# A hybrid decoder layer in which every attention product is made to span the whole TensorE array

## The chip, the cores and the metric

The kernel runs on one core of one Trainium2 chip. The metric is device time in microseconds (us) of one execution; lower is better. Before the change the median of three executions is 1176.98 us (1176.88 to 1177.14).

## The reference

One layer on 256 tokens of width 2048, all in float32. A first projection makes queries (16 heads of 64), keys and values (4 key/value heads, three branches), gates and the input of a convolution. Cut to what matters here:

```python
h = rms_norm(x, mix_norm_g[l]); proj = h @ w_in[l]
q, kv, gate_logits, conv_in = jnp.split(proj, splits, axis=-1)
k_cmp = compress_tokens(kv[:, :, 0, 0], ...)       # blocks of 32 tokens, stride 16, 2-layer MLP
v_cmp = compress_tokens(kv[:, :, 0, 1], ...)
# per query: softmax(q k / 8 + T5 bias) v for three branches, summed with sigmoid gates:
#   compressed blocks (15 of them), selected blocks of 64, sliding window of 512
attn = gc[..., 0:1] * o_cmp + gc[..., 1:2] * o_sel + gc[..., 2:3] * o_win
conv = conformer_conv(conv_in, ...)                 # GLU, 31-tap causal conv, LayerNorm, swish
x = x + jnp.concatenate([attn, conv], axis=-1) @ w_out[l]
x = x + conv_glu_ffn(rms_norm(x, ffn_norm_g[l]), ...)
return rms_norm(x, final_norm_g)
```

With 256 tokens there are four blocks of 64 and up to 16 are selected, and the window is longer than the sequence, so the selected and the window branch both see every earlier token: two plain causal attentions with their own keys and values.

## The kernel before, in words

**Weights.** Every weight matrix comes in chunks of 128x2048 through the queue of SyncE (`wraw`). ScalarE rounds a chunk to the type fp32r (`wh`, line 108), VectorE subtracts that from the original (`wl`, line 111), and each product of the model is the sum of three fp32r products: high with high, high with low, low with high (`mm3`, lines 133 to 135, 256 columns; `mm_rows`, lines 140 to 142, 512 columns). Splits run two chunks ahead of their use.

**Stages.** TensorE first makes the convolution's inputs, then keys and values of the compressed branch, then the two MLPs of the compression (`cmp_in`, line 420: 16 products of 75 columns with 64 weight columns, once for keys and once for values), the keys of the other two branches (`kt_`, line 465), the values (`vt`, lines 485 and 500), and last eight tiles of queries of two heads each (`tile_chunk`, `q_evac` at line 513). The 30 multiply-adds per channel tile of the 31-tap convolution (line 347, "taps" below) are put on VectorE between all this by `fill`, which compares two rough clocks of the planner, one for TensorE and one for VectorE.

**Attention.** There are 32 units, one for each of 16 heads and 2 branches (`units`). `attn_tick` issues one step of a software pipeline over the units; a tick at number n holds, in this order, the value products of unit n-5 (`st_out`), the transposes of unit n-4 (`st_transpose`), the scores of unit n (`st_scores`), and on the other engines the row minima of unit n-1 (VectorE, `st_min`), the reciprocal of the sums (`st_rec`), the evacuation of the transposes, the scaling and the exponential (ScalarE). Four ticks go into each of the query tiles 2 to 7 and into the first chunks of the output projection, between its weight products. These attention products are in plain fp32, which TensorE runs as two instructions each; they use the array in parts. Scores contract over the 64 channels of one head, so they use 64 rows:

```python
nc.tensor.matmul(s[:, :P], qt[h, i, :P], kt_[h, br, i // 4, :P], start=True, stop=True)
```

Values have 64 channels, so their products use 64 columns, and the product with the compressed values (line 630) uses 64 rows. The transposes and all weight products use all 128 rows and 128 columns. The trace writes this as rows*columns behind the operation (64*128, 128*64, 128*128).

The order on each engine is the order in which the Python code issues the work; `hook` is called four times per chunk and pops side work (`steps`, taps, a tick, a piece of a weight split).

Of the kernel before, what the change touches and what calls it, by code (L numbers as in the profile page):

```python
# [45 lines left out]
def hybrid_trunk(ctx: ExitStack, tc: tile.TileContext, a: dict, out: bass.AP):  # L46
# [134 lines left out]
    xt_l = mixp.tile([P, KD, T], F32R, name="xt_l")  # L181


    with ExitStack() as mx:
# [7 lines left out]
        w1 = ap.tile([P, 2, 16, HD], F32, name="w1", tag="w1")  # L192
        w2 = ap.tile([HD, 2, HD], F32, name="w2")
# [43 lines left out]
        rB = ap.tile([P, T], F32, name="rB1")  # L237
# [43 lines left out]
        def tab_rel():  # L281
            pr = bank[6]
            nc.tensor.matmul(pr[:16, :384], rbn, oh[:, P:], start=True, stop=True)
            rtab = wk.tile([16, 384], F32, name="rtab", tag="es", bufs=2)
            nc.vector.tensor_copy(rtab, pr[:16, :384])
            nc.scalar.dma_start(scratch, rtab)
# [32 lines left out]
        def hook(i, ticks=0):  # L319
# [4 lines left out]
            if ticks > i:  # L324
                attn_tick()
            if i >= 2:
                w_pump(1)
            fill(1.0 if ticks > i else 0.8 if cbst["q"] else 2.0)
# [3 lines left out]
        def tile_chunk(ps, ticks=0):  # L332
# [80 lines left out]
        vc = ap.tile([P, 2, 2, HD], F32, name="vc")  # L413
# [3 lines left out]
        def cmp_in(kv):  # L417
            cm[kv] = ph = bank[4 + kv]
            for i in range(16):
                nc.tensor.matmul(ph[:HD, :75], w1[:, kv, i], tok[:, kv, :, i:i + 113:8],  # L420
                                 start=i == 0, stop=i == 15)

        def cmp_sig(kv):
            ph = cm[kv]
            hb = wk.tile([HD, 1], F32, name="hb")
            nc.vector.tensor_copy(hb, ph[:HD, 60:61])
            sgm = wk.tile([HD, 60], F32, name="sgm", bufs=1)
            nc.scalar.activation(sgm, ph[:HD, :60], AF.Sigmoid, bias=hb)
            cm[kv] = ph, hb, sgm

        def cmp_silu(kv):
            ph, hb, sgm = cm[kv]
            cm[kv] = hd = wk.tile([HD, 4, 32], F32, name="hd")
            nc.gpsimd.memset(hd, 0.0)
            nc.vector.scalar_tensor_tensor(hd[:, :, :NCMP], ph[:HD, :60].rearrange("p (h n) -> p h n", h=4),
                                           hb, sgm.rearrange("p (h n) -> p h n", h=4),
                                           op0=OP.add, op1=OP.mult)

        def cmp_out():
            pk, pv = bank[6:]  # L440
            for r in range(2):
                nc.tensor.matmul(pk[64 * r:64 * r + 64, :2 * NCMP], w2[:, 0], cm[0][:, r::2, :NCMP],
                                 start=True, stop=True)
            for j in range(4):
                for q in range(2):
                    nc.tensor.matmul(pv[32 * j:32 * j + 32, q * HD:(q + 1) * HD], cm[1][:, 2 * q + j % 2],
                                     w2[:, 1], start=True, stop=True)

        def cmp_keep():
# [4 lines left out]
            for j in range(4):  # L454
                sl = slice(32 * j, 32 * j + 32)
                nc.vector.tensor_copy(vc[sl, :, j % 2], pv[sl, :2 * HD].rearrange("p (q n) -> p q n", q=2))

        steps.extend((lambda: None, lambda: None, lambda: cmp_in(0), lambda: None, lambda: cmp_sig(0),
                      lambda: (cmp_in(1), cmp_silu(0)), lambda: None, lambda: cmp_sig(1), lambda: None,
                      lambda: cmp_silu(1), lambda: None, cmp_out, lambda: None, cmp_keep))  # L460

        kt_ = ap.tile([P, 2, 2, T], F32, name="kT")
# [5 lines left out]
        vt = ap.tile([P, 2, 2, 256], F32, name="vt")  # L468
# [15 lines left out]
        for t in range(2):  # L484
            nc.scalar.activation(vt[:, t, 0], vb[t][:, :256], AF.Copy, scale=rc[:, t:t + 1])
# [13 lines left out]
        for t in range(2):  # L499
            nc.scalar.activation(vt[:, t, 1], vb[t][:, :256], AF.Copy, scale=rc[:, t:t + 1])  # L500
# [9 lines left out]
        qt = ap.tile([P, 8, T], F32, name="qT", tag="w1")  # L510
# [525 lines left out]
```

## Time and profile before

| | |
|---|---|
| median of three executions | 1176.98 us |
| the profiled execution | 1177.07 us, of which the span of instructions is 1175.3 us |
| granted TensorE clock, mean | 0.997 of full speed |
| TensorE (PE) busy | 1161.2 us, 99% of the span, 7986 products |
| VectorE (DVE) busy | 788.3 us, 67% |
| ScalarE (ACT) busy | 567.4 us, 48% |

The matmul's ends in the trace are modelled and products overlap in it, so what one product costs TensorE is read from the distance between the starts of neighbours, not from its own duration. The chain of waits does that by itself: its entries add up to the span.

### The profile page before, as it was taken

The page shows a single profiled execution, that of the slowest core. Times are in us where ns is not written, and L with a number is a line of the kernel's source. Part 1 is how long each engine was busy: PE and PEld are TensorE (multiplying, and loading weights), DVE is VectorE, ACT ScalarE, POOL GpSimd, SP SyncE. Part 2 cuts the span into 40 slices and gives each one's busy share as a digit, 9 for nine tenths or more (in the row PEclk, how much of TensorE's full clock was granted, in tenths as well). Part 3 has the DMA queues.
Part 4 walks back from the last instruction along what each step waited for, and adds up shares of the span by engine and source line. Part 5 has one row for each costly group of instructions (what it writes and reads, how often), then busy time and mean ns, then how long its engine had stood idle before and what let it go on. Part 6 is the DMA issues. An engine that isn't in the chain of part 4 may idle for free.

```text
span 1175.3 us, 18945 instructions
## 1 busy us (share of the span) xinstructions
PE 1161.2 (99%) x7986; PEld 1058.1 (90%) x7986; DVE 788.3 (67%) x1192; ACT 567.4 (48%) x770; POOL 6.8 (1%) x25
## 2 busy tenths in 40 slices
PE   8999999999999999999999999999999999999997
PEld 8999999777678899999999999999999888888886
DVE  6889889777665666666766666666667654556544
ACT  6544225666655644444453544444444544444443
POOL 1000000000000000000000000000000000000000
PEclk9999999999999999999999999999999999999999
DMA  9575336222245454554445355545544555555551
GB/s 364 217 294 181 144 104 232 73 72 73 71 180 195 163 215 149 211 190 168 174 187 214 144 209 176 190 155 204 199 160 175 218 182 183 185 205 179 179 178 72
DMA packets 32224, 207.60 MB, mean 177 GB/s; under 512 B 3739, under 2 KB 6123, under 8 KB 7948
## 3 DMA queue, kind: packets, MB, share of 16 engines
q1 hardware_dynamic: 28592, 199.64, 47.1%
q10 hardware_dynamic: 3548, 6.76, 1.6%
q8 instruction: 62, 1.02, 0.3%
q14 instruction: 22, 0.18, 0.0%
HBM read 204.27 MB, written 2.12 MB: 176 GB/s over the span
## 4 chain that ended last, share of the span: by engine, by line
PE 95%; DMA 2%; DVE 1%; ACT 1%; issue 1%; SPq 0%; POOLq 0%; DVEq 0%; POOL 0%; ACTq 0%
PE bank L133 19%; PE bank L134 19%; PE bank L135 19%; PE bank L140 9%; PE bank L142 9%; PE bank L141 9%; PE bank L625 2%; PE bank L611 1%; DMA wraw<-in_w_t 1%; PE bank L570 1%; PE bank L569 1%; DMA hb<-in_head 1%; PE bank L420 1%; PE bank L626 1%; PE bank L630 0%
## 5 line engine op out<-in xcount | busy, mean ns | idle before, releaser
L133 PE MATMUL bank<-xt_h,wh 128*128 128x256 f32 x1920 | 548.1, 285 | 2.6 <-ACT wh L233 2.6
L135 PE MATMUL bank<-xt_h,wl 128*128 128x256 f32 x1920 | 544.8, 284 | 0.5 <-DVE wl L111 0.4
L134 PE MATMUL bank<-xt_l,wh 128*128 128x256 f32 x1920 | 544.5, 284 | 0.0
L111 DVE TENSOR_TENSOR wl<-wraw,wh 128x2048 fp32r<-128x2048 f32 (+2 forms) x239 | 421.3, 1784 | 119.0 <-ACT wh L108 118.9
L108 ACT ACTIVATE wh<-wraw 128x2048 fp32r<-128x2048 f32 (+2 forms) x239 | 352.6, 1500 | 141.0 <-PE bank L142 62.5
L133 PEld LDWEIGHTS bank<-xt_h,wh 128*128 128x128 f32 x1920 | 368.9, 192 | 12.2 <-issue 9.0
L135 PEld LDWEIGHTS bank<-xt_h,wl 128*128 128x128 f32 x1920 | 368.9, 192 | 1.2 <-DVE wl L234 0.6
L134 PEld LDWEIGHTS bank<-xt_l,wh 128*128 128x128 f32 x1920 | 369.0, 192 | 0.0
L844 ACT ACTIVATE yt<-u,vecs 128x256 f32<-128x256 f32 x88 | 53.0, 602 | 204.9 <-DVE u L842 204.9
L142 PE MATMUL bank<-wh,gl 128*128 128x512 f32 (+1 forms) x360 | 140.9, 392 | 0.0
L140 PE MATMUL bank<-wh,gh 128*128 128x512 f32 (+1 forms) x360 | 140.9, 392 | 0.0
L141 PE MATMUL bank<-wl,gh 128*128 128x512 f32 (+1 forms) x360 | 140.9, 391 | 0.0
L847 DVE SCALAR_TENSOR_TENSOR yt<-u,vecs,yt 128x255 f32<-128x255 f32 (+1 forms) x176 | 85.1, 484 | 62.3 <-ACT yt L844 59.1
L347 DVE SCALAR_TENSOR_TENSOR y<-us,cw,y 128x256 f32<-128x256 f32 x240 | 101.2, 479 | 0.4 <-ACT y L350 0.3
L142 PEld LDWEIGHTS bank<-wh,gl 128*128 128x128 f32 x360 | 67.9, 189 | 15.7
L141 PEld LDWEIGHTS bank<-wl,gh 128*128 128x128 f32 x360 | 67.9, 188 | 15.7
L140 PEld LDWEIGHTS bank<-wh,gh 128*128 128x128 f32 x360 | 67.9, 188 | 15.7
L842 DVE TENSOR_TENSOR u<-bank,rB 128x256 f32<-128x256 f32 x88 | 36.9, 420 | 27.1 <-PE bank L135 27.1
L836 ACT ACTIVATE gh<-gt 128x1024 fp32r<-128x1024 f32 x22 | 23.3, 1059 | 64.6 <-PE bank L141 64.6
L837 DVE TENSOR_TENSOR gl<-gt,gh 128x1024 fp32r<-128x1024 f32 x22 | 27.0, 1225 | 41.0 <-ACT gh L836 41.0
L879 ACT ACTIVATE sgf<-yt 128x256 f32<-128x256 f32 x44 | 18.4, 418 | 50.3 <-DVE yt L847 50.3
L880 DVE TENSOR_TENSOR gt<-sgf,yt 128x256 f32<-128x256 f32 x44 | 18.7, 426 | 24.5 <-ACT sgf L879 24.5
(171 smaller groups left out, 795.8 us busy)
## 6 DMA issues: line engine op xcount, KB each, us to landing
wraw<-in_w_u SPq DMA_DIRECT2D x88, 1024.0 KB, 4.9
wraw<-in_w_d SPq DMA_DIRECT2D x44, 1024.0 KB, 4.8
wraw<-in_w_t SPq DMA_DIRECT2D x30, 1024.0 KB, 5.0
wraw<-in_w_o SPq DMA_DIRECT2D x16, 1024.0 KB, 4.9
wraw<-in_w_vg SPq DMA_DIRECT2D x4, 608.0 KB, 3.7
hb<-in_head SPq DMA_DIRECT2D x2, 1024.0 KB, 10.9
xr<-in_x SPq DMA_DIRECT2D x2, 1024.0 KB, 16.6
wb<-rel_scratch ACTq DMA_DIRECT2D x1, 2048.0 KB, 13.0
```

What stands on the lines that cost most here:

```text
L108: nc.scalar.activation(h[:, sl], raw[:, sl], AF.Copy)
L111: nc.vector.tensor_sub(l[:, sl], raw[:, sl], h[:, sl].bitcast(F32))
L133: nc.tensor.matmul(ps, wh, xh, start=first, stop=False)
L134: nc.tensor.matmul(ps, wh, xl, start=False, stop=False)
L135: nc.tensor.matmul(ps, wl, xh, start=False, stop=last)
L140: nc.tensor.matmul(ps, xh, wh, start=first, stop=False)
L141: nc.tensor.matmul(ps, xh, wl, start=False, stop=False)
L142: nc.tensor.matmul(ps, xl, wh, start=False, stop=last)
L347: nc.vector.scalar_tensor_tensor(y[:, j], us[:, j, k:k + T], cw[:, j, k:k + 1], y[:, j], op0=OP.mult, op1=OP.add)
L842: nc.vector.tensor_mul(u, bank[:, :T], rB)
L844: nc.scalar.activation(yt, u, AF.Identity, scale=fcw[:, c, 2:3], bias=fcw[:, c, 3:4])
L847: nc.vector.scalar_tensor_tensor(yt[:, d:], u[:, :T - d], fcw[:, c, k:k + 1], yt[:, d:], op0=OP.mult, op1=OP.add)
```

## The change

Five things change.

1. **Scores.** The queries of a head are stored on all 128 partitions, the fp32r high part on one half and the low part on the other (`qs`); the keys are stored twice, once on each half, as a high tile `k_h` and a low tile `k_l`. One fp32r product then contracts over 128 rows and gives (high + low) times high, a second one adds the rest. Both branches lie side by side in the moving operand, so one call serves two units: four products with 256, 256, 512 and 512 columns.
2. **Values** are zero-padded to 128 columns (`vt` has a block of zeros between the two heads), so a unit's value products write all 128 partitions; the compressed values are padded in the same way over rows (`vc`).
3. **Compression.** The first layers for keys and values run as one product with 128 weight columns and 150 moving columns; only two of its four quarters are used.
4. **New copies.** Each key tile takes one VectorE product, six ScalarE copies and two VectorE subtractions on 64 partitions; each query tile two copies and two subtractions beside its evacuation.
5. **Plan.** The planner's price of a tick falls from 2.5 to 1.4. Ticks start in query tile 1 (two of them), stay at four in tiles 2 to 7, six go into the first chunk of the output projection, the rest into its second chunk. The pipeline of ticks and its order are otherwise as they were.

TensorE, one tick inside a query tile. Before (`kT`, `qT` are keys and queries, `es` the transposed probabilities, `e` the probabilities):

```order
L625 MATMUL bank_71<-es,vt 64x256
L626 MATMUL bank_71<-es,vt 64x128
L611 MATMUL bank_70<-ident,e 128x128 x3
L569 MATMUL bank_68<-kT,qT 128x128
L570 MATMUL bank_68<-kT,qT 128x256
L133 MATMUL bank_65<-xt_h,wh 128x256
```

After, a tick that carries scores (the next tick ends behind its transposes):

```order
L659 MATMUL bank_71<-es,vt 128x256
L660 MATMUL bank_71<-es,vt 128x128
L646 MATMUL bank_70<-ident,e 128x128 x3
L604 MATMUL bank_66<-k_h,qs 128x256
L605 MATMUL bank_66<-k_l,qs 128x256
L604 MATMUL bank_68<-k_h,qs 128x512
L605 MATMUL bank_68<-k_l,qs 128x512
L133 MATMUL bank_65<-xt_h,wh 128x256
```

The sequence is the same; the scores of two units stand together, every second tick has none, and the value products write 128 partitions instead of 64.

VectorE, the end of a query tile. Before (`smc`, `pcb` belong to the compressed branch):

```order
L111 TENSOR_TENSOR wl<-wraw,wh 128x1024
L347 SCALAR_TENSOR_TENSOR y<-us,cw,y 128x256 x3
L513 SCALAR_TENSOR_TENSOR qT<-bank_64,rB_191 128x256
L544 TENSOR_REDUCE smc<-ec 128x8
L545 RECIPROCAL smc<-smc 128x8
L546 TENSOR_TENSOR smc<-smc,gates 128x8
```

After:

```order
L111 TENSOR_TENSOR wl<-wraw,wh 128x1024
L348 SCALAR_TENSOR_TENSOR y<-us,cw,y 128x256 x2
L535 SCALAR_TENSOR_TENSOR q_2736<-bank_64,rB 128x256
L539 TENSOR_TENSOR qs<-q_2736,qs 64x256 x2
L570 TENSOR_REDUCE smc<-ec 128x8
L571 RECIPROCAL smc<-smc 128x8
L572 TENSOR_TENSOR smc<-smc,gates 128x8
```

Two subtractions are new behind the evacuation, and each of them reads what ScalarE has just copied; fewer taps stand in the tile (19 in two tiles, where 24 stood).

VectorE, where the taps run out, in the first chunks of the output projection. Before:

```order
L347 SCALAR_TENSOR_TENSOR y<-us,cw,y 128x256 x5
L544 TENSOR_REDUCE smc<-ec 128x8
L545 RECIPROCAL smc<-smc 128x8
L546 TENSOR_TENSOR smc<-smc,gates 128x8
L547 TENSOR_TENSOR pcb<-ec,smc 128x8x15
L633 TENSOR_TENSOR ma_l<-bank_71,ma_h 128x256
L579 ISA e,mn<-bank_69,wb 128x128
L579 ISA mn 128x1
L579 ISA e,mn<-bank_69,wb 128x256
L579 ISA mn 128x1
L662 TENSOR_REDUCE y<-y 128x128
L598 RECIPROCAL lsum<-lsum 128x4
```

After:

```order
L348 SCALAR_TENSOR_TENSOR y<-us,cw,y 128x256 x3
L666 TENSOR_TENSOR ma_l<-bank_71,ma_h 128x256
L614 ISA e,mn<-bank_66,wb 128x128
L614 ISA mn 128x1
L614 ISA e,mn<-bank_69,wb 128x256
L614 ISA mn 128x1
L348 SCALAR_TENSOR_TENSOR y<-us,cw,y 128x256 x18
L633 RECIPROCAL lsum<-lsum 128x4
L634 TENSOR_TENSOR lsum<-lsum,gates 128x4
L695 TENSOR_REDUCE y<-y 128x128 x2
```

Eighteen taps are left when the last row minima are done, and they stand ahead of the reciprocal of the last two units.

The diff, cut to its core (tile declarations, renamed indices and the layout on the host are left out):

```diff
-        def hook(i, ticks=0):
+        def hook(i, ticks={}):
...
-            if ticks > i:
-                attn_tick()
+            if i in ticks:
+                for _ in range(ticks[i]):
+                    attn_tick()
...
-        def cmp_in(kv):
-            cm[kv] = ph = bank[4 + kv]
+        def cmp_in():
             for i in range(16):
-                nc.tensor.matmul(ph[:HD, :75], w1[:, kv, i], tok[:, kv, :, i:i + 113:8],
+                nc.tensor.matmul(bank[4][:, :150], w1[:, i].rearrange("p v d -> p (v d)"), tok[:, :, :, i:i + 113:8],
                                  start=i == 0, stop=i == 15)
...
         for n in range(4):
             tile_chunk(bank[n][:, :T])
-            nc.vector.tensor_mul(kt_[:, n // 2, n % 2], bank[n][:, :T], rB)
+            br, q = divmod(n, 2)
+            k32 = wk.tile([P, T], F32, name="k32", tag="q32", bufs=2)
+            nc.vector.tensor_mul(k32, bank[n][:, :T], rB)
+            for r in range(2):
+                h, o = slice(64 * r, 64 * r + 64), slice(64 - 64 * r, 128 - 64 * r)
+                nc.scalar.activation(k_h[h, r, q, br], k32[h], AF.Copy)
+                nc.vector.tensor_sub(k_l[h, r, q, br], k32[h], k_h[h, r, q, br].bitcast(F32))
+                nc.scalar.activation(k_h[o, r, q, br], k32[h], AF.Copy)
+                nc.scalar.activation(k_l[o, r, q, br], k_l[h, r, q, br].bitcast(F32), AF.Copy)
...
         def q_evac(i, bank):
-            nc.vector.scalar_tensor_tensor(qt[:, i], bank[:, :T], -(HD ** -0.5), rB, op0=OP.mult, op1=OP.mult)
+            q32[i] = wk.tile([P, T], F32, name="q32", tag="q32", bufs=2)
+            nc.vector.scalar_tensor_tensor(q32[i], bank[:, :T], -(HD ** -0.5), rB, op0=OP.mult, op1=OP.mult)
+            for r in range(2):
+                h, o = slice(64 * r, 64 * r + 64), slice(64 - 64 * r, 128 - 64 * r)
+                nc.scalar.activation(qs[h, i % 4, r], q32[i][h], AF.Copy)
+                nc.vector.tensor_sub(qs[o, i % 4, r], q32[i][h], qs[h, i % 4, r].bitcast(F32))
...
+        def st_bank(n):
+            hh = n // 2
+            return bank[2][:, hh % 2 * T:(hh % 2 + 1) * T], bank[4 + hh % 2]
+
         def st_scores(n):
             i, r, br = units[n]
-            h = slice(64 * r, 64 * r + 64)
-            s = bank[4 + n % 2]
-            nc.tensor.matmul(s[:, :P], qt[h, i, :P], kt_[h, br, i // 4, :P], start=True, stop=True)
-            nc.tensor.matmul(s[:, P:384], qt[h, i, P:], kt_[h, br, i // 4], start=True, stop=True)
+            if br:
+                return
+            q, q4 = qs[:, i % 4, r], i // 4
+            for t, s in enumerate(st_bank(n)):
+                sl, ks = slice(t * P, (t + 1) * P), slice(0, (t + 1) * P)
+                nc.tensor.matmul(s, q[:, sl], k_h[:, r, q4, :, ks], start=True, stop=False)
+                nc.tensor.matmul(s, q[:, sl], k_l[:, r, q4, :, ks], start=False, stop=True)
...
         def st_out(n):
             i, r, br = units[n]
             es = US.pop(n)
-            o = bank[7][64 * r:64 * r + 64]
-            c0 = (2 * (i // 4) + r) * HD
+            o, v = bank[7], vt[:, :, br, i // 4, r:r + 2]
             kw = dict(skip_group_check=True)
-            nc.tensor.matmul(o[:, :T], vt[:, 0, br, c0:c0 + HD], es[:, :T], start=br == 0, stop=False, **kw)
-            nc.tensor.matmul(o[:, P:T], vt[:, 1, br, c0:c0 + HD], es[:, T:], start=False, stop=False, **kw)
+            nc.tensor.matmul(o[:, :T], v[:, 0], es[:, :T], start=r + br == 0, stop=False, **kw)
+            nc.tensor.matmul(o[:, P:T], v[:, 1], es[:, T:], start=False, stop=False, **kw)
...
-            clock["pe"] += 2.5
+            clock["pe"] += 1.4
...
+        TICKS = {0: {}, 1: {2: 1, 3: 1}, 2: {0: 1, 1: 1, 2: 1, 3: 1}, 3: {0: 1, 1: 2, 2: 1, 3: 2}}
         for i in range(8):
-            tile_chunk(bank[i % 2][:, :T], ticks=4 if i > 1 else 0)
+            tile_chunk(bank[i % 2][:, :T], TICKS[min(i, 2)])
...
         for n, (qr, g) in enumerate(OUT_ORDER):
-            if n == 2:
+            if n == 1:
+                while cbst["done"] < 4:
+                    step()
                 while tick["n"] < NU + 1:
                     attn_tick()
```

## Rows read from the trace of the kernel before

**Rows 1.** The page's chain that ended last, by engine and by line.

```profile
PE 95%; DMA 2%; DVE 1%; ACT 1%; issue 1%; SPq 0%; POOLq 0%; DVEq 0%; POOL 0%; ACTq 0%
PE bank L133 19%; PE bank L134 19%; PE bank L135 19%; PE bank L140 9%; PE bank L142 9%; PE bank L141 9%; PE bank L625 2%; PE bank L611 1%; DMA wraw<-in_w_t 1%; PE bank L570 1%; PE bank L569 1%; DMA hb<-in_head 1%; PE bank L420 1%; PE bank L626 1%; PE bank L630 0%
```

**Rows 2.** Stretches: start:end, length, busy us per engine, clock, DMA share, GB/s.

```profile
130.00:165.00 35.00, 35.00 (x293) 34.02 (x293) 25.85 (x57) 8.19 (x11) 0.00 (x0) 1.00 0.31 106
165.00:198.00 33.00, 33.00 (x262) 33.00 (x261) 31.80 (x61) 14.42 (x25) 0.00 (x0) 1.00 0.61 219
231.10:263.10 32.00, 32.00 (x198) 23.77 (x198) 23.36 (x80) 21.23 (x64) 0.13 (x1) 1.00 0.19 66
291.00:320.00 29.00, 29.00 (x138) 18.78 (x137) 21.18 (x65) 19.25 (x60) 0.00 (x0) 1.00 0.16 43
320.00:334.00 14.00, 12.61 (x62) 8.25 (x60) 4.81 (x10) 8.73 (x21) 0.00 (x0) 1.00 0.56 214
```

**Rows 3.** Timeline of TensorE, one tick: start us, duration us, what.

```profile
236.00 0.28 PE L134 MATMUL bank<-xt_l,wh 128*128 128x256 f32 x1
236.12 0.28 PE L135 MATMUL bank<-xt_h,wl 128*128 128x256 f32 x1
236.33 0.65 PE L625 MATMUL bank<-es,vt 128*64 128x256 f32 x2
236.81 0.38 PE L626 MATMUL bank<-es,vt 128*64 128x128 f32 x2
237.12 0.55 PE L611 MATMUL bank<-ident,e 128*128 128x128 f32 x3
237.60 0.48 PE L569 MATMUL bank<-kT,qT 64*128 64x128 f32 x2
237.92 0.59 PE L570 MATMUL bank<-kT,qT 64*128 64x256 f32 x2
238.45 0.39 PE L133 MATMUL bank<-xt_h,wh 128*128 128x256 f32 x1
238.67 0.28 PE L134 MATMUL bank<-xt_l,wh 128*128 128x256 f32 x1
```

**Rows 4.** Timeline of TensorE, transposes among 512-column products, later in the kernel.

```profile
390.32 0.39 PE L142 MATMUL bank<-wh,mc_l 128*128 128x512 f32 x1
390.55 0.60 PE L765 MATMUL bank<-ident,x 128*128 128x128 f32 x4
390.91 0.48 PE L140 MATMUL bank<-wh,mc_h 128*128 128x512 f32 x1
391.22 0.40 PE L141 MATMUL bank<-wl,mc_h 128*128 128x512 f32 x1
```

**Rows 5.** The chain in order of time: start us, its share in us, what.

```profile
132.03 4.51 PE bank L420 x32
...
201.27 0.81 PE bank L524 x8
...
202.50 0.43 PE bank L570 x2
```

**Rows 6.** Timeline of TensorE, the next tick, with the compressed values.

```profile
240.55 0.38 PE L626 MATMUL bank<-es,vt 128*64 128x128 f32 x2
240.86 0.70 PE L630 MATMUL bank<-pct,vc 64*128 64x256 f32 x2
241.49 0.33 PE L611 MATMUL bank<-ident,e 128*128 128x128 f32 x1
```

**Rows 7.** TensorE's waits: engine, line, releaser, total us, times, longest.

```profile
PE bank L611 <- ACT ck L690: 1.4, 1, 1.4
```

**Rows 8.** Groups by line in 231.1 to 263.1: count, busy us, mean ns, idle before.

```profile
L347 DVE SCALAR_TENSOR_TENSOR y<-us,cw,y 128x256 f32<-128x256 f32 x24 | 10.2, 480 | 0.0
...
L605 ACT ACTIVATE e<-e,lsum 128x256 f32<-128x256 f32 x8 | 4.0, 499 | 0.0
...
L616 ACT ACTIVATE es<-bank 128x384 f32<-128x384 f32 x8 | 3.9, 490 | 9.1 <-PE bank L611 9.1
...
L598 DVE RECIPROCAL lsum<-lsum 128x4 f32<-128x4 f32 x4 | 0.7, 178 | 4.2 <-ACT e L590 4.1
```

More of the change, by code (lines that the diff above doesn't have):

```diff
@@ L181, in hybrid_trunk @@
     xt_l = mixp.tile([P, KD, T], F32R, name="xt_l")
+    rB = mixp.tile([P, T], F32, name="rB")
     with ExitStack() as mx:
@@ L191, in hybrid_trunk @@
         cw = ap.tile([P, 8, TAPS + 3], F32, name="cw")
-        w1 = ap.tile([P, 2, 16, HD], F32, name="w1", tag="w1")
-        w2 = ap.tile([HD, 2, HD], F32, name="w2")
+        w1 = ap.tile([P, 16, 2, HD], F32, name="w1", tag="w1")
+        w2 = ap.tile([P, HD], F32, name="w2")
         def load_small():
@@ L283, in tab_rel @@
             nc.tensor.matmul(pr[:16, :384], rbn, oh[:, P:], start=True, stop=True)
-            rtab = wk.tile([16, 384], F32, name="rtab", tag="es", bufs=2)
+            rtab = wk.tile([16, 384], F32, name="rtab", tag="e", bufs=4)
             nc.vector.tensor_copy(rtab, pr[:16, :384])
@@ L412, in hybrid_trunk @@
         nc.gpsimd.memset(kc, 0.0)
-        vc = ap.tile([P, 2, 2, HD], F32, name="vc")
+        vc = ap.tile([P, 2, 2, 2, HD], F32, name="vc")
         nc.gpsimd.memset(vc, 0.0)
         cm = {}
-        def cmp_in(kv):
-            cm[kv] = ph = bank[4 + kv]
+        def cmp_in():
             for i in range(16):
-                nc.tensor.matmul(ph[:HD, :75], w1[:, kv, i], tok[:, kv, :, i:i + 113:8],
+                nc.tensor.matmul(bank[4][:, :150], w1[:, i].rearrange("p v d -> p (v d)"), tok[:, :, :, i:i + 113:8],
                                  start=i == 0, stop=i == 15)
         def cmp_sig(kv):
[L424 to L429, printed above, removed]
-        def cmp_silu(kv):
[L432 to L436, printed above, removed]
+            h = slice(64 * kv, 64 * kv + 64)
+            ph = bank[4][h, 75 * kv:75 * kv + 75]
+            hb = wk.tile([P, 1], F32, name="hb")
+            nc.vector.tensor_copy(hb[h], ph[:, 60:61])
+            sgm = wk.tile([P, 60], F32, name="sgm", bufs=2)
+            nc.scalar.activation(sgm[h], ph[:, :60], AF.Sigmoid, bias=hb[h])
+            cm[kv] = h, ph, hb, sgm
+        def cmp_silu(kv):
+            h, ph, hb, sgm = cm[kv]
+            cm[kv] = hd = wk.tile([P, 4, 32], F32, name="hd")
+            nc.gpsimd.memset(hd[h], 0.0)
+            nc.vector.scalar_tensor_tensor(hd[h, :, :NCMP], ph[:, :60].rearrange("p (h n) -> p h n", h=4),
+                                           hb[h], sgm[h].rearrange("p (h n) -> p h n", h=4),
                                            op0=OP.add, op1=OP.mult)
@@ L445, in cmp_out @@
                 for q in range(2):
-                    nc.tensor.matmul(pv[32 * j:32 * j + 32, q * HD:(q + 1) * HD], cm[1][:, 2 * q + j % 2],
-                                     w2[:, 1], start=True, stop=True)
+                    nc.tensor.matmul(pv[32 * j:32 * j + 32, q * HD:(q + 1) * HD], cm[1][HD:, 2 * q + j % 2],
+                                     w2[HD:], start=True, stop=True)
         def cmp_keep():
@@ L651, in attn_tick @@
                 if 0 <= n - d < NU:
-                    assert f is not st_scores or n // 8 < cbst["q"]
+                    assert f is not st_scores or n // 4 in q32
                     f(n - d)
@@ L712, in conf_split @@
             if j0 == 0:
-                cf["o"] = (ap.tile([P, 8, T], F32R, name="mc_h", tag="us"), ap.tile([P, 8, T], F32R, name="mc_l"))
+                cf["o"] = (ap.tile([P, 8, T], F32R, name="mc_h", tag="us"), ap.tile([P, 8, T], F32R, name="mc_l", tag="mc_l"))
             sl = slice(j0, j0 + 4)
@@ L741, in hybrid_trunk, with out_part @@
         x2 = None
-        def out_part(ws, qr, g, t):
+        def out_part(n, ws, qr, g, t):
             wh, wl = ws
@@ L802, in hybrid_trunk @@
         dg = mixp.tile([P, 2, P], F32, name="dg2")
-        rB = mixp.tile([P, T], F32, name="rB")
         def x2_rstd(t):
```

51 lines of the change are left out of this document (28 added, 23 removed).

## The prediction

> **What bounds the kernel now.** I read the chain of waits first. TensorE holds 95% of it, nearly all of it in weight products that the change leaves alone; the lines that it touches hold about 7% [rows 1]. So TensorE's own time is what counts, and the question is what the attention products cost it. The stretches say the same of the stage where they are: in two query tiles TensorE is busy for all of 32.0 us at a granted clock of 1.00 (the upper level, 2.4 GHz), while VectorE has 23.4 us of work and ScalarE 21.2 us [rows 2]. Third comes one tick in TensorE's timeline, where the starts of neighbours give the price of each piece [rows 3]. A weight product of 256 columns takes 0.12 us there, from start to start.
>
> **Array switches.** From the start of L135 to the start of L134 behind the tick 2.55 us pass [rows 3]; two weight products of 0.12 are in that, so the tick takes 2.31 us. The bare price of its contents comes from stretches where nothing changes shape. Four transposes between 512-column products take, with the product behind them, from 390.55 to 391.22, that is 0.67 us; a 512-column product alone takes 0.23 (390.32 to 390.55), so an fp32 pass of 128 columns is 0.11 us [rows 4], and one of 256 columns 0.215 (0.43 for two) [rows 5]. The tick holds 2 x 0.215 + 2 x 0.108 for the values, 3 x 0.108 for the transposes, 2 x 0.108 + 2 x 0.215 for the scores: 1.61 us. The other 0.70 us stand where the shape of the array changes: weight product (128 rows by 128 columns) to values (128 by 64), to transposes (128 by 128), to scores (64 by 128), back to the weight product; four changes of about 0.17 us. Entering transposes from a weight product of the same shape costs nothing [rows 4], nor does leaving them, so it is the shape and not the change from fp32r to fp32 that costs. Afterwards all of it has one shape. Over 32 units: 32 x 0.70 = 22.4 us. Where the compressed values follow, from 240.86 to 241.49 pass 0.63 us for two passes worth 0.43 [rows 6]; eight of these give 8 x 0.20 = 1.6 us more.
>
> **Scores.** Two units cost 2 x 0.646 = 1.29 us of bare passes now. Afterwards they are two fp32r products of 256 and two of 512 columns, 2 x 0.12 + 2 x 0.23 = 0.70 us. Sixteen pairs: 20.7 - 11.2 = 9.5 us.
>
> **Padded values.** The passes have as many columns as before, so they take the same time; only the weights are 128 wide instead of 64. Products of 32 columns behind loads of 128 take 0.10 us each [rows 5], so such a load takes at most 0.10 us; the transposes have loads of that width and run at 0.11 us a pass [rows 4], so the loads hide behind 128 columns, and I take 0 (bounds: 0 to 2 x 0.10 x 32 = 6.4 us, if those behind the two shorter passes came out whole). By the Trainium skill, "TensorE: Matmul & The Clock Gate", section "LDWEIGHTS (loading the stationary operand)", a load goes by its columns, P/1.2 ns: my estimate from it is 107 instead of 53 ns, and were none hidden, four loads in 32 units would take 6.8 us from the sum; the 0.10 us of the row agrees with the duration.
>
> **Compression.** 32 passes of 75 columns take 4.51 us, 0.141 each [rows 5], more than 128 neighbouring columns take (0.11). The moving columns lie eight elements apart. If the time goes by such columns, the 32 passes of 150 take as long as the 64 passes now (9.0 us) and nothing is saved; if it goes by passes, 4.5 us are saved. I take 0, since 75 columns that cost more than 128 are most simply slow columns, and add 0.6 us for the four shape changes around the two visits (at 0.17). By the Trainium skill, "SBUF — State Buffer", section "Door 1: The DMA port swizzle", full rate needs accesses that fall in the same line of 16 bytes, four fp32, and steps beyond that pay for each access: by it too the sum is 0, without it 4.5 us.
>
> **A wait that goes.** TensorE waits 1.4 us once for ScalarE's copy of a convolution mean [rows 7], because that column range shares a bank with the transposes. In the new order the means come behind the last tick: 1.4 us.
>
> TensorE alone: 22.4 + 1.6 + 9.5 + 0.6 + 1.4 = 35.5 us.
>
> **What comes back as waits.** The tick shrinks from 2.31 to (0.646 + 0.324 + 0.35) = 1.32 us, so two tiles shrink from 32.0 to 32.0 - 8 x 0.99 - 0.2 = 23.9 us. VectorE's work there [rows 2]: 23.4, less 5 taps of 0.43, plus 4 half-height subtractions, at the tap's price for want of a row, so 22.9. ScalarE's: 21.2 plus 4 copies at 0.50 = 23.2 [rows 8]. All three engines stand within 1 us. ScalarE's queue used to wait 9.1 us there for transposes, and VectorE's 4.2 us for the exponentials [rows 8]; that slack is what the change spends. Three places can stop TensorE:
> - Tile ends: VectorE evacuates, ScalarE copies, VectorE subtracts, and everything behind that in both queues (row minima, the next weight split, the evacuation of transposes) waits. Hidden, it costs 0; with both copies exposed VectorE needs 22.9 + 2 = 24.9, 1.0 more than TensorE per two tiles, 3 us over six tiles. I take 2.
> - The first output chunk has six ticks among 24 products, twice two in a row, and a seventh follows. A second tick's value products need the evacuation of the transposes just issued. The one exposed step in the trace cost 1.4 us [rows 7]; three of them give 0 to 4.2. I take 2.
> - Eighteen taps, 18 x 0.43 = 7.7 us, stand on VectorE ahead of the last reciprocal, and ScalarE's scaling and TensorE's transposes of the last two units are behind it. TensorE still has two ticks without scores (2 x 0.97) and some nine 512-column products (2.1) before it asks. The cover is 4 us: 0 to 3.7. I take 2.
>
> Copies of the keys: in 130 to 165 VectorE is busy 25.9 of 35 us and ScalarE 8.2 [rows 2], so 12 more operations of 0.43 and 24 copies of 0.50 fit; the next stretch has VectorE at 31.8 of 33, and a lag of 2 or 3 us is carried through it by weight splits that run two chunks ahead. I take 0 (bounds 0 to 3). DMA is busy 0.16 to 0.61 of the time and moves the same bytes.
>
> **Sum.** 35.5 - 6 = 29.5 us off the profiled execution's 1177.07 us (the span of 1175.3 and 1.8 around it; the runs' median of 1176.98 is the same within 0.1): 1147.6 us. With the bounds of the waits, 0 to 10.9, the forecast itself spans 1141.6 to 1152.5.
>
> **Rivals.**
> *VectorE and ScalarE become the bound of attention.* For: work of 22.9 and 23.2 against 23.9 us, in queues that take their work in order; against: in 165 to 198 VectorE already runs at 96% without stopping TensorE [rows 2]. If the 4.2 us per two tiles that VectorE now waits for exponentials stay, VectorE needs 27.1, 3.2 over TensorE, 9.6 over six tiles; with the upper ends of the other two places (7.9) that is 1141.6 + 17.5 = 1159.1. Such runs lie between 1152.5 and 1160.
> *The compression's time goes by passes.* 4.5 us more: 1143.1. For it is only that no row shows two counts of columns at that step.
> *The change does not free the array.* If going between fp32r and fp32, or writing through padded weights, cost the same 0.17 us, three of four changes per tick would stay, 0.52 x 32 = 16.8 us: 1147.6 + 16.8 less the waits that longer ticks would cover (6) is 1158.4. Rows 4 speak against it.
> *Slower.* ScalarE's queue sets the pace of each tick: transposes, evacuation, scaling, next transposes as one loop, exposed in every tick. The place is the wait of the transposes for the scaling; the price is the 1.4 us of the one exposed step [rows 7]. Over 37 ticks that is 51.8 us against a gain of 35.5, so 1193.4; it decides from 0.96 us per tick on. Against it: a loop of one tick needs evacuation and scaling, 0.49 + 0.39 + 0.50 at most, while a tick with its twelve weight products lasts 1.32 + 1.4 = 2.7 us.
>
> **How the numbers follow.** Forecast 66% (1147.6; own range 1141.6 to 1152.5); VectorE and ScalarE as the bound 17% (1152.5 to 1160); compression by passes 8% (1143.1); array not freed 5% (1158.4); slower 4% (1193). A range of 1140 to 1158 leaves out the slower case, most of the array case, a few points of the first rival at its far end and a few of the second with no wait at all: about 2 in 10. About 0.2% (2.4 us) is what a measurement of this kernel can tell from no change. Every case but the last is faster by more than that, and I keep 1% for a mixture of several bad ends: faster 0.95, same 0.01, slower 0.04.
>
> **What would show it.** Right: one tick with scores of about 1.65 us and one without of about 1.0 between weight products in TensorE's timeline; value products marked 128*128 with two passes in 0.65 us together; the stretch of the query tiles 2 to 7 shorter by some 24 us; TensorE's waits on evacuations and probabilities, near absent now, adding up to about 6 us around the first two output chunks and at tile ends; VectorE and ScalarE over 90% busy there; the compression's products still near 9 us. Wrong: starts still 0.2 us late at the edges of a tick (the array), or waits above 11 us in all (VectorE and ScalarE), or a compression of 4.5 us.

## The result, and the profile after

| | before | changed |
|---|---|---|
| median, four executions each | 1177.06 us | 1171.26 us (1169.61 to 1172.36) |
| profiled execution | 1177.07 us | 1169.61 us |
| TensorE busy | 1161.2 us | 1136.2 us |
| VectorE busy | 788.3 us | 797.3 us |
| ScalarE busy | 567.4 us | 582.9 us |

The ratio is 0.9949 with a 95% interval of 0.9937 to 0.9961. The kernel is faster by 5.8 us, half a per cent, where 29.5 were forecast, and the time lies outside the range. TensorE is busy for 25 us less (busy time counts modelled ends, so this is not yet its gain), and the chain shows what took its place. The page's chain that ended last, by engine and by line:

```profile
PE 82%; DVE 11%; ACT 3%; DMA 2%; issue 1%; SPq 0%; DVEq 0%; POOLq 0%; POOL 0%; ACTq 0%
PE bank L133 17%; PE bank L135 17%; PE bank L134 17%; PE bank L140 9%; PE bank L142 9%; PE bank L141 9%; DVE y L348 4%; DVE wl L111 3%; DMA wraw<-in_w_t 1%; DMA hb<-in_head 1%; DVE e L614 1%; PE bank L421 1%; ACT wh L108 1%; PE bank L659 1%; ACT e L625 0%
```

In [rows 1] TensorE held 95% and VectorE 1%; now they hold 82% and 11%, and the first lines of VectorE on the path are the convolution's taps (L348) and the weights' low parts (L111), neither of them touched by the change. The stretches say where (start:end, length, busy us of TensorE, weight loads, VectorE, ScalarE, GpSimd, clock, DMA share, GB/s; those of before are [rows 2]):

```profile
165.00:198.00 33.00, 28.57 (x216) 27.65 (x216) 31.47 (x62) 17.48 (x32) 0.00 (x0) 1.00 0.53 181
204.00:284.00 80.00, 72.40 (x529) 67.21 (x528) 68.90 (x240) 66.10 (x199) 0.38 (x3) 1.00 0.23 80
291.00:320.00 29.00, 23.52 (x118) 19.29 (x117) 23.72 (x70) 18.71 (x57) 0.00 (x0) 0.94 0.10 37
304.00:306.00 2.00, 1.05 (x6) 0.71 (x6) 1.64 (x7) 1.21 (x5) 0.00 (x0) 1.00 0.57 135
306.00:309.40 3.40, 3.40 (x11) 2.94 (x12) 3.40 (x11) 2.26 (x7) 0.00 (x0) 0.51 0.54 229
```

Before, TensorE had no gap in the first four stretches of [rows 2]. Now it lacks 4.4 us in 165 to 198 (the value stage), 7.6 us in 204 to 284 (six query tiles), and 5.5 us in 291 to 320 (the first output chunks), where the clock also stands at its half level (0.51, 1.2 GHz) for 3.4 us, behind 2 us in which TensorE was busy for only 1.05. TensorE's waits by line (total us, times, longest), without those at the start of the kernel; all of them are new:

```profile
PE bank L646 <- ACT e L640: 4.1, 2, 2.6
PE bank L515 <- DVE wl L111: 4.0, 3, 1.8
PE bank L578 <- DVE pcb L573: 3.7, 3, 1.4
...
PE bank L659 <- ACT es L651: 2.0, 6, 0.8
PE bank L550 <- DVE q L535: 1.5, 1, 1.5
PE bank L663 <- ACT pct L580: 1.1, 1, 1.1
```

These six lines alone add up to 16.4 us; the forecast had named more than 11 us of waits as a sign that it was wrong.

The length of the tick came out as forecast. One tick with scores in TensorE's timeline (start us, duration us), which answers to [rows 3]:

```profile
244.25 0.28 PE L135 MATMUL bank<-xt_h,wl 128*128 128x256 f32 x1
244.37 0.59 PE L659 MATMUL bank<-es,vt 128*128 128x256 f32 x2
244.80 0.38 PE L660 MATMUL bank<-es,vt 128*128 128x128 f32 x2
245.02 0.49 PE L646 MATMUL bank<-ident,e 128*128 128x128 f32 x3
245.26 0.37 PE L604 MATMUL bank<-k_h,qs 128*128 128x256 f32 x1
245.47 0.28 PE L605 MATMUL bank<-k_l,qs 128*128 128x256 f32 x1
245.59 0.39 PE L604 MATMUL bank<-k_h,qs 128*128 128x512 f32 x1
245.82 0.39 PE L605 MATMUL bank<-k_l,qs 128*128 128x512 f32 x1
246.05 0.28 PE L133 MATMUL bank<-xt_h,wh 128*128 128x256 f32 x1
```

From 244.37 to 246.05 are 1.68 us (1.65 foreseen), and the values start 0.12 us behind the weight product, as one weight product does behind another: at that edge no change of shape is left. Where the time went is a matter of waits, so I took the starts of the first weight product of each stage from the traces; the differences below are between such starts:

| stretch | before | changed | keys late | keys, queries late | taps last | half taps, means held | fastest order |
|---|---|---|---|---|---|---|---|
| value stage | 24.9 | 30.3 | 24.9 | 24.9 | 30.4 | 27.5 | 24.9 |
| query tiles 2 to 7 | 89.4 | 80.0 | 79.6 | 74.4 | 80.0 | 71.1 | 74.4 |
| first output chunk | 16.3 | 22.0 | 22.0 | 22.2 | 23.3 | 20.6 | 17.2 |
| second output chunk | 17.5 | 14.5 | 15.8 | 14.5 | 9.7 | 11.3 | 10.6 |
| third and fourth | 18.9 | 11.6 | 11.6 | 11.6 | 12.3 | 11.6 | 14.1 |
| whole (median) | 1177.1 | 1171.3 | 1165.0 | 1160.8 | 1167.3 | 1152.0 | 1152.9 |

(us; the columns to the right are the experiments below, and each column is one profiled execution. What follows the fourth output chunk takes 835.3 to 836.7 us in the runs of this table, so the stretches hold nearly all of the difference. The kernel before has its ticks in other chunks, and the fastest order has one of the first output chunk's in the next, so for these two the rows of the output chunks compare only as a sum.)

### The profile page after: what moved, and what is told of

It is laid out like the page before. It is cut to its first block, busy times and chain, and to the rows that moved or that the text cites. A ratio compares the mean times of both kernels' runs of the same rounds, so it can differ in the third digit from the quotient of the medians.

```text
span 1167.8 us, 18821 instructions
## 1 busy us (share of the span) xinstructions
PE 1136.2 (97%) x7890; PEld 1056.6 (90%) x7890; DVE 797.3 (68%) x1216; ACT 582.9 (50%) x810; POOL 7.6 (1%) x26
## 4 chain that ended last, share of the span: by engine, by line
PE 82%; DVE 11%; ACT 3%; DMA 2%; issue 1%; SPq 0%; DVEq 0%; POOLq 0%; POOL 0%; ACTq 0%
PE bank L133 17%; PE bank L135 17%; PE bank L134 17%; PE bank L140 9%; PE bank L142 9%; PE bank L141 9%; DVE y L348 4%; DVE wl L111 3%; DMA wraw<-in_w_t 1%; DMA hb<-in_head 1%; DVE e L614 1%; PE bank L421 1%; ACT wh L108 1%; PE bank L659 1%; ACT e L625 0%
## 5 line engine op out<-in xcount | busy, mean ns | idle before, releaser
L111 DVE TENSOR_TENSOR wl<-wraw,wh 128x2048 fp32r<-128x2048 f32 (+2 forms) x239 | 421.2, 1782 | 120.4 <-ACT wh L108 120.2
L348 DVE SCALAR_TENSOR_TENSOR y<-us,cw,y 128x256 f32<-128x256 f32 x240 | 101.0, 477 | 0.6 <-ACT y L351 0.3
L142 PEld LDWEIGHTS bank<-wh,gl 128*128 128x128 f32 x360 | 67.8, 188 | 15.8
L141 PEld LDWEIGHTS bank<-wl,gh 128*128 128x128 f32 x360 | 67.8, 188 | 15.8
L140 PEld LDWEIGHTS bank<-wh,gh 128*128 128x128 f32 x360 | 67.8, 188 | 15.8
L872 ACT ACTIVATE gh<-gt 128x1024 fp32r<-128x1024 f32 x22 | 23.3, 1059 | 64.6 <-PE bank L141 64.6
L915 ACT ACTIVATE sgf<-yt 128x256 f32<-128x256 f32 x44 | 18.4, 418 | 49.7 <-DVE yt L883 49.7
L916 DVE TENSOR_TENSOR gt<-sgf,yt 128x256 f32<-128x256 f32 x44 | 18.7, 425 | 23.9 <-ACT sgf L915 23.9
```

The source lines that it names most:

```text
L111: nc.vector.tensor_sub(l[:, sl], raw[:, sl], h[:, sl].bitcast(F32))
L140: nc.tensor.matmul(ps, xh, wh, start=first, stop=False)
L141: nc.tensor.matmul(ps, xh, wl, start=False, stop=False)
L142: nc.tensor.matmul(ps, xl, wh, start=False, stop=last)
L348: nc.vector.scalar_tensor_tensor(y[:, j], us[:, j, k:k + T], cw[:, j, k:k + 1], y[:, j], op0=OP.mult, op1=OP.add)
```

## The experiments

The diffs in this section are shortened.

My first theory was that VectorE is late from the keys on; the rival was that the copies through ScalarE and the loop of a tick set the pace, whatever VectorE's load.

**Value stage: the copies of the keys.** This is the chain in order of time (start us, share in us), from the last product of a key tile on:

```profile
143.35 0.43 DVE k L471
143.79 0.02 issue
143.81 0.43 ACT k_h L474
144.24 0.02 issue
144.26 0.43 DVE k_l L475
144.69 0.02 issue
144.72 0.42 ACT k_l L477
...
146.05 0.43 ACT k_l L477
```

The same steps follow once more for the other half of the tile, to 146.47. Each queue stands while the other works: 3.1 us for a key tile in which VectorE does three operations of 0.43. The experiment issues the same operations sorted by engine, each group in a later gap of the next weight tile.

```diff
-  for r in range(2):          # behind each key tile
-      ACT k_h[h]; DVE k_l[h]; ACT k_h[o]; ACT k_l[o]
+  late[0].append(k_high)      # gap 0 of the next tile: ScalarE, four
+  late[1].append(k_low)       # gap 1: VectorE, two
+  late[2].append(k_low2)      # gap 2: ScalarE, two
```

> The changed kernel with the 4 x 3 copies and subtractions of each of the four key tiles issued in later gaps of the next weight tile, sorted by engine (first ScalarE's high parts, then VectorE's low parts, then ScalarE's copies of these), so that neither queue waits for the other in the middle. Theory VectorE is late: its lag into the value stage goes, 3 to 5.4 us less, 1166 to 1168 us. Rival, the lag comes from the taps alone: within 1 us of the changed kernel (1171).

Measured: 1164.95 us (1164.87 to 1165.94), ratio to before 0.9899 (0.9882 to 0.9915), a us better than expected. The value stage has no wait left, with the same work in it:

```profile
165.00:198.00 33.00, 33.00 (x260) 32.92 (x260) 32.30 (x66) 19.34 (x34) 0.00 (x0) 1.00 0.65 230
```

So the 5.4 us lost there came from the order of the copies, not from their number: VectorE is busy for 32.3 of 33 us and stops nobody.

**Fewer taps.** Half of the taps left out, so that part of the convolution is missing, in the changed kernel and, as a control, in the kernel before.

```diff
-  side.append([lambda k=k: tap(k) for k in range(TAPS - 1)])
+  side.append([lambda k=k: tap(k) for k in range(0, TAPS - 1, 2)])
```

> The changed kernel with every second tap of the convolution left out (15 of 30 stay; so part of the convolution is missing). That takes 8 x 15 x 0.43 = 52 us of work off VectorE and nothing off TensorE or ScalarE. Theory VectorE is late: the waits in the value stage (5.4 us against the kernel before), much of the 11 us lost in the query tiles and the 18 taps ahead of the last units go, so about 1171 - 18 = 1153 us (1148 to 1158). Rival, the latency of ScalarE's copies and of the tick's loop sets the pace: VectorE has room and TensorE waits all the same, 1166 us or more.

> Control: the kernel before with every second tap of the convolution left out. TensorE is busy throughout there, so both theories expect the time of the kernel before within 2 us (1175 to 1178); if it falls by more, a shorter VectorE queue is worth something by itself and the other run has to be read less that.

Measured: 1160.92 us (1160.91 to 1162.27), and 1176.14 (1175.96 to 1176.31) for the control, which is what was expected of it. For the first, neither expectation held. The value stage gained 2.8 us and the second output chunk 4.8, as the theory wanted, but the query tiles took 82.3 us. The waits say why this run can't be read there:

```profile
PE bank L659 <- ACT es L651: 3.4, 5, 1.4
PE bank L646 <- ACT ck L723: 3.2, 2, 1.9
```

Line 723 copies the convolution's mean: with the taps gone early, its sums and means moved into the query tiles. At this point I took the tiles for a matter of the handshake alone, and expected the following run accordingly: the same, with the means kept where they are in the changed kernel.

```diff
-  if not side and cbst["q"] and "b" not in cf:
+  if not side and tick["n"] > 32 and "b" not in cf:
```

> The changed kernel with every second tap left out (part of the convolution is missing), as in the first run of that kind (1160.9 us), but with the sums and means of the convolution held back to where they stand in the changed kernel, so that only VectorE's load differs. Theory now: the amount of VectorE's work matters in the value stage and ahead of the last units, but in the query tiles the two queues wait for each other at tile ends whatever the amount: the six tiles stay at 78 us or more (80.0 in the changed kernel), and the whole is about 1171 - 3 (value stage) - 5 (last units) = 1163 us. Rival, VectorE's amount of work sets the tiles: they fall to 74 us or less, and the whole to 1157 or less.

Measured: 1151.97 us (1151.28 to 1152.99), ratio 0.9786 (0.9772 to 0.9801). I was wrong: the six tiles took 71.1 us, the rival's result. Groups by line in the six tiles (count, busy us, mean ns, idle before), first of the changed kernel, then of this run:

```profile
L348 DVE SCALAR_TENSOR_TENSOR y<-us,cw,y 128x256 f32<-128x256 f32 x57 | 24.6, 478 | 0.0
L539 DVE TENSOR_TENSOR qs<-q,qs 64x256 fp32r<-64x256 f32 x12 | 5.0, 420 | 3.1 <-ACT qs L538 2.9
L538 ACT ACTIVATE qs<-q 64x256 fp32r<-64x256 f32 x12 | 5.0, 416 | 6.4 <-DVE q L535 6.3
```

```profile
L540 DVE TENSOR_TENSOR qs<-q,qs 64x256 fp32r<-64x256 f32 x12 | 5.0, 420 | 5.3 <-ACT qs L539 5.2
L539 ACT ACTIVATE qs<-q 64x256 fp32r<-64x256 f32 x12 | 4.9, 409 | 1.4 <-DVE q L536 1.3
```

Here no tap stands in the tiles (the first group is absent). VectorE still waits for ScalarE's copy, longer even (5.3 us), and it costs nothing, because VectorE has 45.2 us of work in 71.1. ScalarE's wait for the query falls from 6.4 to 1.4 us; no taps stand ahead of the query's evacuation now. With 57 taps VectorE has 68.9 us of work: 97% of the 71.1 us that TensorE needs.

**Query tiles: the copies of the queries.** The same sorting for the queries, on top of that for the keys: ScalarE's two copies in gap 0 of the next tile, VectorE's two subtractions in gap 1.

```diff
-  for r in range(2): ACT qs[h]; DVE qs[o]     # behind each query tile
+  late[0].append(q_high); late[1].append(q_low)
```

> The changed kernel with the key copies spread over the next tile (as in the run before, 1165.0 us) and also the query copies and subtractions: ScalarE's two in the next tile's first gap, VectorE's two in its second, where both queues waited for each other at each tile end. Theory VectorE and ScalarE wait for each other at tile ends: 0.3 to 0.5 us for each of eight tiles, 1161 to 1163 us. Rival, the pace of a query tile is set by the ticks' own loop and the compressed branch: within 1 us of 1165.

Measured: 1160.75 us (1158.95 to 1161.61), ratio 0.9859 (0.9844 to 0.9873). The tiles fall from 79.6 to 74.4 us with 56 taps in them. Both queues' waits are nearly gone:

```profile
L351 DVE SCALAR_TENSOR_TENSOR y<-us,cw,y 128x256 f32<-128x256 f32 x56 | 24.2, 478 | 0.0
L561 DVE TENSOR_TENSOR qs<-q,qs 64x256 fp32r<-64x256 f32 x12 | 5.0, 420 | 0.4
L557 ACT ACTIVATE qs<-q 64x256 fp32r<-64x256 f32 x12 | 5.0, 416 | 0.8 <-DVE q L551 0.3
```

The loss in the tiles thus comes from two things together: a VectorE without slack and a handshake in order in both queues. Without the taps the tiles take 71.1 us with the old order of the copies, and 71.5 in the last run below, which has the copies sorted as well: there the order is worth nothing. With the taps it is worth 5.2 of the 8.5 us, and 3.3 stay.

**Probabilities a gap earlier.** TensorE waits 3.7 us for `pcb`, which VectorE makes behind the query's copies.

```diff
-  (None, cmp_scores, cmp_exp, None, cmp_probs, cmp_tr)
+  (None, cmp_scores, cmp_exp, cmp_probs, None, cmp_tr)
```

> The changed kernel with one step moved: the probabilities of the compressed branch are worked out one gap earlier, ahead of the tile's end, instead of behind the next tile's query copies. TensorE waits three times for them, 3.7 us in all. If these are waits of their own, 1171.3 - 3.7 = 1167.6 us (1166.5 to 1168.5). Rival, VectorE is the bound and the wait only moves: 1170 or more.

Measured: 1173.56 us (1171.93 to 1174.88), 2.3 us slower than the changed kernel. The wait for `pcb` is gone and the one for the evacuated transposes has grown from 2.0 to 6.0 us:

```profile
PE bank L659 <- ACT es L651: 6.0, 9, 1.5
```

So the wait moved; it was not one of its own. (In this execution the clock also fell to its half level three times, so not all of the 2.3 us need be waits.) With the query copies spread it goes by itself (it is not among the listed waits of that run).

**Left-over taps.** The chain in the changed kernel, in order of time, and VectorE's step that the last two units wait for:

```profile
306.27 7.12 DVE y L348 x18
313.39 0.10 DVE lsum L633
313.49 0.02 issue
313.52 0.17 DVE lsum L634
...
313.77 0.81 ACT e L640 x2
314.58 0.04 issue
314.63 0.44 PE bank L646 x2
```

```diff
-  if n == 1: fill(1e9)                      # all taps, ahead of the ticks
+  fill(1e9 if tick["n"] > 33 else ...)      # behind the last reciprocal
```

> The changed kernel with the 18 left-over taps issued behind the last reciprocal instead of ahead of it; nothing else. Theory: the wait of the last two units (2.6 us) and what the half clock behind it cost (3.4 us at half speed, 1.7 us) go: 1167 us (1166 to 1168). Rival, VectorE's amount of work is the bound: it returns as a wait for a weight's low part or for the convolution's mean, 1170 or more.

Measured: 1167.33 us (1166.51 to 1168.16), ratio 0.9917 (0.9902 to 0.9931). The second output chunk falls from 14.5 to 9.7 us, with the clock at 1.00 from 300 to 317. The time is as expected, but only half of the theory is shown. The wait is gone; the half level of the clock is not, it stands elsewhere in this execution, once in query tile 2 and once in the first output chunk, which takes 1.3 us longer (stretches as above):

```profile
213.30:216.70 3.40, 3.40 (x16) 3.21 (x15) 2.98 (x11) 2.26 (x9) 0.00 (x0) 0.50 0.00 0
288.40:291.80 3.40, 3.40 (x12) 2.72 (x11) 2.62 (x12) 3.15 (x9) 0.00 (x0) 0.50 0.35 147
```

So the profiled executions differ by only 1.6 us (1169.61 and 1168.02), where the medians differ by 3.9.

**All of it, and the double ticks.** The four changes together, with one tick to a gap in the first two output chunks:

```diff
-  3: {0: 1, 1: 2, 2: 1, 3: 2}
+  3: {0: 1, 1: 1, 2: 1, 3: 1}
-  ob = [bank[0:2], bank[2:4], ...]; all ticks with a minimum ahead of n == 1
+  ob = [bank[0:2], bank[2:4][::-1], ...]; they are ahead of its second half
```

Then the same without the move of the probabilities; then that with this besides:

```diff
-  m == 3: (cmp_scores, cmp_exp, None, cmp_probs, cmp_tr)
+  m == 3: (None, cmp_scores, cmp_exp, cmp_probs, cmp_tr)
+  attn_tick()                       # at n == 1
   while cbst["done"] < 4: step()
+  attn_tick()
```

> The changed kernel with all of these (key and query copies spread, probabilities a gap earlier, left-over taps last) and the ticks of the first two output chunks one to a gap instead of two: the second output half takes its two banks in the other order, so that its first half can begin while scores are still being read. By addition of the single waits: 1171.3 - 6.3 (keys) - 2 (queries) - 3.7 (probabilities) - 4.3 (taps) - 4 (double ticks) = 1151 us (1147 to 1155). Rival, VectorE or ScalarE is the bound by the sum of its work: the parts don't add, 1158 or more.

> The changed kernel with key and query copies spread, the left-over taps last and one tick to a gap in the first two output chunks; the probabilities of the compressed branch stay where they were, since moving them cost 2 us. From the four together (1156.6) less 2 to 2.5: 1154 us (1152.5 to 1155.5). If the probabilities did no harm with the query copies spread, 1156 to 1157.

> As the run beside it, with the compressed branch of the last two tiles begun one gap later (TensorE waits 1.5 us there for the last query) and a tick on either side of its transposes. Theory: the two waits there (1.5 and 1.9 us) go, 1151 us (1150 to 1152.5). Rival: the waits move to the evacuations, within 0.7 us of the run beside it.

Measured: 1156.56 us (1156.43 to 1158.15); 1154.85 (1154.09 to 1155.48); 1152.87 (1152.84 to 1153.18), ratio 0.9794 (0.9779 to 0.9808). The first expectation, by addition, was 5 us too good: 1.7 were the probabilities, and about 2 came back in the third and fourth output chunk (13.7 us against 11.6), where the taps now stand ahead of the convolution's means. The rest of the 5 us was not placed. The second came out in its range; the third a little above its own, and 2.0 us below the run beside it, so its theory holds and its rival does not. The last is the fastest complete kernel here, 18.4 us faster than the changed one with the same products on TensorE.

**GpSimd for the low parts.** The fastest order, with one engine exchanged:

```diff
-  nc.vector.tensor_sub(qs[o, ...]); nc.vector.tensor_sub(k_l[h, ...])
+  nc.gpsimd.tensor_sub(qs[o, ...]); nc.gpsimd.tensor_sub(k_l[h, ...])
```

> As the last run, with the subtractions for the low parts of keys and queries (24 of half height, about 0.43 us each on VectorE, 10 us) on GpSimd, which is idle. Theory: VectorE's queue is what the ticks wait for in places: 1 to 3 us less than the last run. Rival: GpSimd's subtractions are late for the scores, or its traffic slows VectorE: no gain, or some us more.

Measured: 1152.93 us (1152.78 to 1152.96), no gain, as the rival had it. Groups by line from 130 to 300, with the subtractions on VectorE and on GpSimd:

```profile
L352 DVE SCALAR_TENSOR_TENSOR y<-us,cw,y 128x256 f32<-128x256 f32 x151 | 64.2, 480 | 0.2
```

```profile
L352 DVE SCALAR_TENSOR_TENSOR y<-us,cw,y 128x256 f32<-128x256 f32 x151 | 72.2, 532 | 0.1
```

```profile
L562 POOL TENSOR_TENSOR qs<-q,qs 64x256 fp32r<-64x256 f32 x16 | 13.2, 827 | 97.0 <-ACT qs L558 69.2 <-issue 27.2
```

VectorE is rid of 24 operations of 0.42, 10 us, and its taps take 8 us longer.

**TensorE's own parts.** The kernel before with the padded values and compressed values alone:

```diff
-  o = bank[7][64 * r:64 * r + 64]; values vt[:, t, br, c0:c0 + HD]
+  o = bank[7]; values vt[:, t, br, i // 4, r:r + 2]   # zeros beside them
```

and the fastest order with half of the taps and the means held, by the two edits shown above (with 33 for 32).

> The kernel before with the zero-padded values and compressed values alone; scores and the compression stay as they were. A tick keeps two of its four changes of shape (into and out of the scores), so 32 x 0.35 = 11.2 us plus 8 x 0.20 = 1.6 us go from TensorE: 1164 us if nothing waits, as both theories expect, since no copy is added and ticks stay over 1.9 us long. If the loop through ScalarE is near its limit already, 1168 or more.

> The fastest order so far (key and query copies spread, left-over taps last, one tick to a gap, the last compressed branch a gap later; 1152.9 us) with every second tap left out, so that part of the convolution is missing and VectorE has about 52 us less to do; the means stay behind the ticks. What is left is TensorE's own time. If the forecast's term for TensorE alone was right (35.5 us), the time comes to 1177.1 - 35.5 = 1141.6, and 1143 to 1145 with the two or three short waits that no tap causes. If TensorE's own gain was only some 32 us, 1146 to 1148. If it stays at 1151 or more, VectorE was not what held the fastest order.

Measured: 1167.45 us (1167.36 to 1167.5), ratio 0.9917 (0.9903 to 0.9932): 9.6 us from two of four shape changes, where 12.8 were expected. A tile of four ticks went from 15.8 to 14.5 us, 1.3 where 4 x 0.35 + 0.2 = 1.6 were expected. One tick of this run, from the weight product ahead of it to the second one behind it, as in [rows 3]:

```profile
234.35 0.28 PE L135 MATMUL bank<-xt_h,wl 128*128 128x256 f32 x1
...
236.61 0.28 PE L134 MATMUL bank<-xt_l,wh 128*128 128x256 f32 x1
```

That is 2.26 us against 2.55, so the two changes around the values cost 0.29 together, 0.14 each, and 0.41 of the tick's 0.70 is left for the two around the scores. The expectation had split the 0.70 evenly; over 32 units this is 1.9 of the 3.2 us that were missing.

The fastest order with half of the taps took 1146.41 us (1146.28 to 1146.82), ratio 0.974 (0.9724 to 0.9756), with 2.1 us of attention's waits left:

```profile
PE bank L682 <- ACT es L674: 1.5, 3, 0.5
...
PE bank L140 <- ACT pct L603: 0.6, 1, 0.6
```

So TensorE's own gain is about 1177.1 - 1146.4 + 2.1 = 33 us, an estimate: the list counts a wait only from the modelled end of the product ahead of it.

## Why the prediction was wrong

Point by point:
- **Array switches, scores, padded values**: right. The tick has the length foreseen, no edge between weight products and values is left, and padded values cost nothing: two passes of 256 columns, from 244.37 to 244.80, take the same 0.43 us. The sum of 0.70 us for four changes of shape holds; that each costs about 0.17 does not (0.14 at the values, 0.20 at the scores).
- **Compression**: right. The chain has 8.89 us for the 32 products of L421, from 132.27 on, in place of two times 4.51 [rows 5]: 0.278 us for 150 columns against 0.141 for 75, so the time goes by the columns and nothing is saved. That rival is out.
- **A wait that goes**: right. TensorE no longer waits for a convolution mean in the changed kernel.
- **TensorE alone, 35.5 us**: 2 to 3 us too large (33 in the last run). The runs do not place this difference.
- **What comes back as waits, 6 us** (bounds 0 to 10.9): this is the step that failed. The terms, as forecast and as measured: copies of the keys 0 against 5.4 (30.3 - 24.9); tile ends 2 against 8.9 for all that the six tiles lost (80.0 - 71.1); the first output chunk 2 against some 4.2 (its waits: 1.5 for the last query, 1.1 for the compressed probabilities, 0.8 for an evacuation, 0.8 for minima); the eighteen taps 2 against 4.8 (14.5 - 9.7), the half level of the clock included, which a run without that wait had elsewhere. Together 23 us, 17 more than forecast. Three of the four lie beyond their own bounds (3, 3 and 3.7; the sum of 10.9 leaves the keys' 3 out), and the first output chunk stands at its own (4.2). With TensorE's 2 to 3 that makes some 20 of the 22.0 us between the profiled 1169.6 and 1147.6.

Why it was so small: the prediction priced each wait as one exposed latency at one place. The amounts of work were right: VectorE has 68.9 us in six tiles, 23.0 in two, where 22.9 were forecast. At 97% of TensorE's time that leaves next to nothing to make up for a wait in order, and the forecast bounded the loss with 1 us for two tiles where it is about three. The argument that VectorE at 96% in 165 to 198 had stopped nobody [rows 2] was true of a queue without handshakes, and is true again once these are sorted. The keys' bound of 3 us failed likewise: "fit" counted the busy time of each engine, not the time in which each stood for the other.

One of the prediction's signs was also too high. It has the six query tiles shorter by some 24 us, which takes each at 16; before, they took 89.4 us, since the first two of them, while the ticks start, take 10.7 and 14.2. Even with TensorE almost alone they are shorter by 18.3 (89.4 - 71.1). That these 71.1 us lie close to three times the forecast's 23.9 is in part luck: a later pair of tiles takes 24.7 there.

The rival *VectorE and ScalarE become the bound* named the engines, with 17%, and its 9.6 us over six tiles is close to the 8.9 lost. But the wait that it priced is not the one that came: VectorE waits for exponentials for only 1.7 us in all six tiles of the changed kernel, against 4.2 in two tiles before. It left the keys out as well, and ended at 1159.1. ScalarE's half of it did not come: with 64.2 us of work in the tiles of 71.1 us TensorE waits for its evacuations for 0.7 us there. The rival *not freed* is out by the tick, the rival *slower* by the time. No case of the prediction gives 1171.

Open: the 3.3 us that the fastest order still loses in the query tiles (74.4 against 71.1). VectorE's longest wait there is another hand-over, the high half of the attention output, which ScalarE copies (`ma_h`); with the query copies sorted it stands as it does here, and no run moved it:

```profile
L688 DVE TENSOR_TENSOR ma_l<-bank,ma_h 128x256 fp32r<-128x256 f32 x5 | 2.1, 424 | 3.9 <-ACT ma_h L687 3.9
```

Open too is what of the first output chunk's loss the double ticks made, since bank order and spread of ticks were tried together only.

## What to carry to other kernels

When TensorE is made faster inside a pipeline, take the load of every other engine in the new, shorter stretch first. A high load alone did no harm here (32.3 of 33 us), nor did a handshake in order alone (45.2 of 71.1 us); together they cost 5.4 us in the value stage and 8.5 in six query tiles, of which sorting the copies gave back all and 5.2. At such a load, count each wait of that engine as exposed. Two engines that hand halves of a tile to and fro in order take the sum of both; sort such work by engine and put one group to a gap. Work that nobody needs soon (here the taps) belongs behind the small operations that others wait for.

## What the runs showed of the hardware

- With 64x256 subtractions on GpSimd (827 ns each, 419 on VectorE) VectorE's taps took 532 ns instead of 480 on average, over 151 of them, so what is moved to GpSimd is nearly paid back on VectorE.
- TensorE's clock at its half level (0.51 in 306.0 to 309.4) costs, as an estimate, half of these 3.4 us, 1.7. It came in the changed kernel behind 2 us in which TensorE was busy for 1.05. Where it comes differs between executions: with the left-over taps last it stands at 213.3, behind 2 us with TensorE busy for 1.13, and at 288.4; the changed kernel, which is the same up to the first of these places, was busy for the same 1.13 us of 2 there (211.2 to 213.2) and kept the full clock. The kernel before, the padded values alone, half of the taps without the means held (1160.9 us, with waits of up to 1.9), and the orders of 1152.9 and 1146.4 us show 1.00 through all of attention.
